# Rows of a norm's reciprocals by four transposes, and another order in the last half of the final norm

## The chip, the cores and the metric

The kernel runs on one core of one Trainium2 chip. A NeuronCore has TensorE (matmuls and transposes into PSUM; the profile calls it PE, and its weight loads PEld), VectorE (DVE), ScalarE (ACT), GpSimd (POOL) and SyncE (SP, which here only issues DMAs). The metric is the device time of one execution in microseconds, as the median of several runs. Before the change the median of 3 runs is 1398.92 us (1397.98 to 1399.54).

## The reference

A decoder trunk of two layers over 512 tokens and a model width of 1024: a gated DeltaNet layer, a channel mixer, a shared K/V projection with sliding-window attention, a second channel mixer, and a final norm. What the change touches is the norm, whose divisors are made four times after the first layer's mixer (the K/V and the query norm share theirs):

```python
def rmsnorm(x, w):
    xf = x.astype(jnp.float32)
    y = xf * lax.rsqrt(jnp.mean(xf * xf, axis=-1, keepdims=True) + EPS)
    return (y * w.astype(jnp.float32)).astype(x.dtype)
```

It divides each token by the root of the mean of its 1024 squares and weighs each feature. Ahead of a projection the kernel multiplies the weighed but undivided activations and divides the product afterwards, token by token; at the end the output itself is the norm.

## The kernel before, in words

Activations lie turned: `h[0]` to `h[7]`, each 128 features on the partitions and the 512 tokens along the row (`T` = 512, `NC` = 4 blocks of 128 tokens, `P` = 128). Every large product is made of three matmuls a block of 128 features (L165, L166, L167: upper part times upper part, and two mixed ones), into one of three PSUM banks tagged `d`. Other banks are tagged `g` (two), `s` (two) and `p` (one).

The reciprocals of the roots. `rstd_cols` squares the eight rows on ScalarE (L860), adds them on VectorE into `acc` (L864), and sums over the 128 partitions with four small matmuls against a column of ones (L867), so that the 512 sums stand as four columns of 128 tokens; root (L869, ScalarE) and reciprocal (L870, VectorE) give `rt`, 128 x 4. The products, however, have the tokens along the row. `rstd_rows` therefore turns the four columns into a row that is the same on all partitions: VectorE multiplies the identity by each column (L876), which gives four diagonal blocks in the tile `st3` (`st` in the profile), and one matmul with a block of ones (L883) sums each column of that diagonal over the partitions; ScalarE copies the bank to the tile `p6s` (L885), and VectorE multiplies the products by it (L911 in the channel mixer, L1284 in the attention). This is done three times: in the first channel mixer (near 525 us), in the attention (near 887 us) and in the second channel mixer (near 1037 us). `st3` is at other times a third buffer for weights of the down projections, which are loaded from L1032 by SP's queue, and on whose parts VectorE first makes sums (L1067).

The down projections and the DeltaNet's output projection are made in a form of seven block products (L1051 to L1053), for which VectorE adds and subtracts parts of weights and of activations first; in the output projection these activations come back from DRAM (`yd`, L1152 on SP) into the tiles `sz` and `zl`.

The final norm. `ffn(1, ..., last=True)` leaves out the last 128 features of its down projection and calls `final`, which interleaves them with the norm. The first seven rows are weighed (L1207) and their squares added into `acc` there, and the four transposes of the first 512 features of each block of tokens (`front`) are made before. The last row's product comes in two halves of 256 tokens (`CUTS`). Each half, once its product is added (L1258), is finished by `finish(u)`: the last row is weighed (L1233) and squared (L1234, `sq7`), the other four rows of each block are transposed (`back`), the squares summed in columns (L1239, first `acc`, then `sq7`, for each block), root and reciprocal taken (L1240, L1241), and the two halves of each block of output rows scaled by `rt`, the front one on VectorE (L1248), the back one on ScalarE (L1246), and sent out from SP's queue (L1249), 256 KB each.

The order of the work on each engine is set by a scheduler from the order in the code, priorities and buffers; `behind(later, earlier)` ties one instruction behind another on an engine without a wait, and `together` keeps several instructions of TensorE in one piece.

Of the kernel before, what the change touches and what calls it, by code (L numbers as in the profile page):

```python
# [11 lines left out]
AF = mybir.ActivationFunctionType  # L12
ALU = mybir.AluOpType
# [4 lines left out]
P = 128  # L18
T = 512
NC = T // P  # L20
D = 1024
KD = D // P
EPS = 1e-6
# [21 lines left out]
def kernel(  # L45
# [27 lines left out]
    V, S, G, PE, SP = nc.vector, nc.scalar, nc.gpsimd, nc.tensor, nc.sync  # L73
# [9 lines left out]
    def nm(s):  # L83
        cnt[0] += 1
        return f"{s}_{cnt[0]}"
# [24 lines left out]
    def row(tag, dt=F32, n=T):  # L110
        return main.tile([P, n], dt, tag=tag, bufs=ROWS[tag], name=nm(tag))
# [4 lines left out]
    def bank(tag):  # L116
        return psum.tile([P, T], F32, tag=tag, bufs=BANKS[tag], name=nm(tag))

    def const(shape, dt=F32, s="c"):
        return cp.tile(list(shape), dt, name=nm(s))  # L120
# [58 lines left out]
    def behind(later, earlier):  # L179
        info = mybir.DependencyInfo(mybir.DependencyClass.NoSync, mybir.DependencyReason.DATA)  # L180
        tc.add_manual_dep(later.ins, earlier.ins.name, info, reason="order of issue")
# [3 lines left out]
    def together(makes, *after):  # L185
        first = None
        for make in makes:
            if first is None:
                first = make()
                for a in after:  # L190
                    behind(first, a)
            else:
                with tc.high_priority(JUMP):
                    behind(make(), first)
# [16 lines left out]
    for i in range(2):  # L211
        cs = slice(HQK * P + i * P, HQK * P + (i + 1) * P)
# [4 lines left out]
    ident = const([P, P], s="ident")  # L217
# [3 lines left out]
    ones = const([P, P], s="ones")  # L221
    V.memset(ones[:], 1.0)
    epsc = const([P, 1], s="eps")
    V.memset(epsc[:], EPS)
    onec = ones[:, 0:1]
# [4 lines left out]
    def columns(parts, n, s, q=SP, tag="acc", place="g"):  # L230
        st = row(tag, n=P)
        r = 0
        for ap in parts:
            k = ap.shape[0]
            q.dma_start(st[r : r + k, :], ap)
            r += k
        ps = bank(place)
        PE.transpose(ps[:, :n], st[:n, :], ident[:n, :n])
        t = const([P, n], s=s)
        V.tensor_copy(t[:], ps[:, :n])  # L240
        return t
# [11 lines left out]
        q=S,  # L253
# [11 lines left out]
    xh, xl = [], []  # L265
    for k in range(KD):
        ps = bank("g") if k % 2 else bank("s")
# [68 lines left out]
    for c in range(NC):  # L336
        cs = slice(c * P, (c + 1) * P)
        V.tensor_tensor_scan(R[32:48, cs], ones[32:48, 0:P], sp_r[32:48, cs], 0.0, op0=ALU.mult, op1=ALU.add)
    for c in range(NC):
        cs = slice(c * P, (c + 1) * P)  # L340
# [38 lines left out]
    def hc(ap):  # L379
# [36 lines left out]
    onw_c = columns(  # L416
        [
            fconv_rows[0, 128:132, :],
            fconv_rows[1, 128:132, :],
            a_out_norm_w,  # L420
            final_norm_w.rearrange("(r c) -> r c", c=P),
        ],
        17,
        "onwc",
        tag="f",
# [351 lines left out]
    for pos, word in enumerate(" ".join(ORDER).split(), 1):  # L777
        name, _, later = word.partition("@")
        a, n = name[0], [int(d) for d in name[1:]]
# [33 lines left out]
    def nxt(role, tags):  # L813
        turn[role] = turn.get(role, -1) + 1
        return tags[turn[role] % len(tags)]

    def r2(role, dt=F32):
        return row(nxt(role, ROLES[role]), dt)
# [4 lines left out]
    def third_stage():  # L823
        return main.tile([P, 6, 256], F32, tag="st3", bufs=1, name=nm("st3"))
# [25 lines left out]
    for m in range(KD):  # L850
        x3 = xrows[m].rearrange("p (c e) -> p c e", c=NC)
        SP.dma_start(x3, x[0, :, m * P : (m + 1) * P].rearrange("(c p) e -> p c e", p=P))
        pt = bank("g")
        turn_row(pt, xrows[m])
        S.copy(hT[m], pt[:])
    def rstd_cols(h):
        acc = None
        for k in range(KD):
            sq = r2("sum" if acc is None else "hsq")
            S.activation(sq[:], h[k], AF.Square)  # L860
            if acc is None:
                acc = sq
            else:
                V.tensor_tensor(acc[:], acc[:], sq[:], op=ALU.add)  # L864
        ps = bank("g")
        for c in range(NC):
            PE.matmul(ps[:, c : c + 1], acc[:, c * P : (c + 1) * P], onec, start=True, stop=True)  # L867
        rt = const([P, NC], s="rt")
        S.activation(rt[:], ps[:, 0:NC], AF.Sqrt, bias=epsc[:, 0:1], scale=1.0 / D)  # L869
        V.reciprocal(rt[:], rt[:])  # L870
        return rt

    def rstd_rows(h):
        rt = rstd_cols(h)
        dg = third_stage()[:, 0:2, :].rearrange("p k c -> p (k c)")
        V.tensor_tensor(  # L876
            dg[:].rearrange("p (c t) -> p c t", c=NC),
            ident[:].unsqueeze(1).to_broadcast([P, NC, P]),
            rt[:].unsqueeze(2).to_broadcast([P, NC, P]),
            op=ALU.mult,  # L880
        )
        ps = bank("g")
        PE.matmul(ps[:], ones[:], dg[:], start=True, stop=True)  # L883
        r = r2("rstd")
        S.copy(r[:], ps[:])  # L885
        return r
# [11 lines left out]
    def ffn(l, h, last=False):  # L898
        wup, wdn = ffn_w_up[l], ffn_w_down[l]
        uh, ul = normed(h, NFFN + 8 * l)  # L900
        rs = rstd_rows(h)

        def tap(j, t):
# [274 lines left out]
    for m2 in range(KD // 2):  # L1178
        srcs = [tiles_of(a_w_out[0], 1024 * u, 8, 256 * m2) for u in range(2)]
        sts = [load_stage(a_w_out[0], 1024 * u, 8, 256 * m2) for u in range(2)]  # L1180
        if m2 < 2:
            for j in range(2):
                m = 2 * m2 + j
                ps = bank("d")
# [15 lines left out]
    def final(h, last_down):  # L1200
        hw, acc = [], None
        for k in range(KD):
            t = r2("xh")
            hw.append(t)
            if k == KD - 1:
                break
            V.tensor_scalar(t[:], h[k], onw_c[:, 9 + k : 10 + k], None, op0=ALU.mult)  # L1207
            sq = r2("sum" if acc is None else "hsq")
            S.activation(sq[:], h[k], AF.Square)
            if acc is None:  # L1210
                acc = sq
            else:
                V.tensor_tensor(acc[:], acc[:], sq[:], op=ALU.add)

        def turned(hf, c, tag):
            pt = bank(tag)
            for k in range(4):
                PE.transpose(pt[:, k * P : (k + 1) * P], hw[4 * hf + k][:, c * P : (c + 1) * P], ident[:])
            return pt

        CUTS = [(0, 2), (2, 4)]
        parts = [bank("d") for _ in CUTS]
        S.activation(warm[:], acc[:, 0:1], AF.Sqrt)
        front = [turned(0, c, t) for c, t in enumerate(["s", "s", "p", "g"])]
        h7, w7 = h[KD - 1], hw[KD - 1]
        sq7 = r2("hsq")
        rt = const([P, NC], s="rt")
        ts = [slice(a * P, b * P) for a, b in CUTS]

        def finish(u):  # L1230
            c0, c1 = CUTS[u]
            cs = slice(c0, c1)
            V.tensor_scalar(w7[:, ts[u]], h7[:, ts[u]], onw_c[:, 16:17], None, op0=ALU.mult)  # L1233
            S.activation(sq7[:, ts[u]], h7[:, ts[u]], AF.Square)  # L1234
            back = [turned(1, c, "s" if u and c % 2 else "d") for c in range(c0, c1)]
            ps = bank("g")
            for c in range(c0, c1):
                for x in (acc, sq7):
                    PE.matmul(ps[:, c : c + 1], x[:, c * P : (c + 1) * P], onec, start=x is acc, stop=x is sq7)  # L1239
            S.activation(rt[:, cs], ps[:, cs], AF.Sqrt, bias=epsc[:, 0:1], scale=1.0 / D)  # L1240
            V.reciprocal(rt[:, cs], rt[:, cs])  # L1241
            for c in range(c0, c1):
                for hf, pt in enumerate((front[c], back[c - c0])):
                    y = r2("xl")
                    if hf:
                        S.activation(y[:], pt[:], AF.Copy, scale=rt[:, c : c + 1])  # L1246
                    else:
                        V.tensor_scalar(y[:], pt[:], rt[:, c : c + 1], None, op0=ALU.mult)  # L1248
                    SP.dma_start(out[0, c * P : (c + 1) * P, hf * T : (hf + 1) * T], y[:])  # L1249

        n = len(CUTS)
        for u in range(n):
            ps = parts[u][:, 0 : ts[u].stop - ts[u].start]
            last_down(ps, ts[u], 0)
            if u > 0:
                finish(u - 1)
            last_down(ps, ts[u], 1)
            V.tensor_tensor(h7[:, ts[u]], h7[:, ts[u]], ps, op=ALU.add)  # L1258
        finish(n - 1)


    Vp = main.tile([P, NC, 256], F32, tag="m32", bufs=1, name="Vp")
# [281 lines left out]
```

## Time and profile before

| | us |
|---|---|
| median of 3 runs | 1398.92 (1397.98 to 1399.54) |
| the profiled execution | 1399.55 |
| its span, from the first to the last instruction | 1397.4 |
| TensorE busy | 1374.6 |
| VectorE busy | 1144.3 |
| ScalarE busy | 765.6 |

The profile takes one execution apart. Rows of the timeline give the start and the length in us, engine, source line, operation, output tile and input tiles, shapes and, in brackets, how long the engine had been idle and what ended that. Lengths of matmuls overlap, so that what one costs is read from the distance of starts. `xN` at the end of a row counts instructions that were merged into it; a float32 matmul (not a transpose) is two instructions.

### The profile page before, as it was taken

How to read it: one execution, taken by the hardware profiler on the slowest of the kernel's cores; microseconds unless marked ns; L12 is line 12 of the kernel's file. 1: busy time of each engine (PE TensorE's matmuls, PEld its weight loads, DVE VectorE, ACT ScalarE, POOL GpSimd, SP SyncE). 2: the span in 40 equal slices, each digit the busy share in tenths (PEclk: the TensorE clock that was granted, in tenths of full speed). 3: DMA queues.
4: the chain of work that ended last, by engine and by line, in shares of the span. 5: the costliest groups of instructions: out<-in, count | busy, mean ns of one | idle time of the engine just before them, and what ended most of it. 6: DMA issues, size and time to landing. Idle time of an engine off the chain costs nothing.

```text
span 1397.4 us, 22194 instructions
## 1 busy us (share of the span) xinstructions
PE 1374.6 (98%) x8514; PEld 1171.0 (84%) x8514; DVE 1144.3 (82%) x2153; ACT 765.6 (55%) x1482; POOL 15.2 (1%) x33
## 2 busy tenths in 40 slices
PE   7999999999999999999999999999999999999998
PEld 5788887888887898888988889877788889988897
DVE  4896896978967998879968899788668889878996
ACT  7766465757557455444344445677545444444543
POOL 1000000000100000000000000000000000000000
PEclk9999999999999999999999999999999999999999
DMA  5234154162567334221343223312132221432222
GB/s 162 83 114 134 50 173 141 64 197 91 171 192 225 127 119 140 94 88 52 130 151 121 76 84 114 121 62 69 61 113 91 91 95 63 146 106 80 96 76 76
DMA packets 164029, 154.97 MB, mean 111 GB/s; under 512 B 24340, under 2 KB 150869, under 8 KB 163925
## 3 DMA queue, kind: packets, MB, share of 16 engines
q1 hardware_dynamic: 161666, 153.37, 34.3%
q8 instruction: 67, 1.10, 0.3%
q10 hardware_dynamic: 2259, 0.20, 0.1%
q14 instruction: 37, 0.30, 0.1%
HBM read 136.74 MB, written 15.75 MB: 109 GB/s over the span
## 4 chain that ended last, share of the span: by engine, by line
PE 90%; DVE 4%; ACT 3%; DMA 2%; issue 1%; SPq 0%; DVEq 0%; ACTq 0%
PE d L165 19%; PE d L167 19%; PE d L166 19%; PE g L201 2%; PE d L1053 2%; PE d L1051 2%; PE d L1052 2%; PE s L1053 1%; PE s L1051 1%; PE s L1052 1%; PE d L1307 1%; PE d L1311 1%; PE d L1309 1%; PE g L1053 1%; PE g L1052 1%; PE g L1051 1%
## 5 line engine op out<-in xcount | busy, mean ns | idle before, releaser
L166 PE MATMUL d<-xl,whi 128*128 128x512 f32 x1128 | 443.0, 395 | 0.0
L165 PE MATMUL d<-xh,whi 128*128 128x512 f32 x1128 | 442.6, 395 | 0.4 <-DVE va L1284 0.3
L167 PE MATMUL d<-xh,wlo 128*128 128x512 f32 x1128 | 442.5, 394 | 0.0
L135 ACT CAST whi<-stage 128x1024 fp32r<-128x1024 f32 (+2 forms) x238 | 231.6, 977 | 224.9 <-PE d L166 129.3
L136 DVE TENSOR_TENSOR wlo<-stage,whi 128x1024 fp32r<-128x1024 f32 (+2 forms) x238 | 268.1, 1129 | 51.8 <-ACT whi L135 50.5
L165 PEld LDWEIGHTS d<-xh,whi 128*128 128x128 f32 x1128 | 211.7, 188 | 44.8 <-DVE va L1284 0.7
L167 PEld LDWEIGHTS d<-xh,wlo 128*128 128x128 f32 x1128 | 211.7, 188 | 44.5 <-DVE wlo L136 0.7
L166 PEld LDWEIGHTS d<-xl,whi 128*128 128x128 f32 x1128 | 211.7, 188 | 43.4 <-issue 0.7
L283 DVE SCALAR_TENSOR_TENSOR acc<-d,cwc,acc 128x511 f32<-128x511 f32 (+2 forms) x96 | 70.2, 738 | 5.2 <-ACT acc L280 4.5
L933 ACT ACTIVATE dt<-dt 128x512 f32<-128x512 f32 x44 | 27.8, 632 | 80.2 <-DVE dt L916 80.2
L911 DVE TENSOR_TENSOR sz<-d,p6s 128x512 f32<-128x512 f32 x58 | 39.9, 688 | 37.6 <-PE d L167 35.3
L916 DVE SCALAR_TENSOR_TENSOR va<-sz,fcw,va 128x511 f32<-128x511 f32 (+1 forms) x58 | 43.4, 747 | 1.7 <-ACT va L914 0.9
L916 DVE SCALAR_TENSOR_TENSOR dt<-sz,fcw,dt 128x511 f32<-128x511 f32 (+1 forms) x58 | 43.3, 746 | 1.7 <-ACT dt L914 0.9
L564 DVE TENSOR_TENSOR sT<-sT,p6s 64x31 f32<-64x31 f32 (+15 forms) x124 | 40.8, 329 | 1.6
L1376 ACT ACTIVATE dt<-dt,sm 128x256 f32<-128x256 f32 (+1 forms) x64 | 30.1, 471 | 21.5 <-DVE sm L1359 21.5
L558 DVE TENSOR_TENSOR p6s<-sN,sT 64x31 f32<-64x31 f32 (+15 forms) x124 | 40.6, 327 | 1.5
L135 ACT CAST whi<-st 128x768 fp32r<-128x768 f32 (+1 forms) x30 | 23.8, 792 | 31.5 <-PE g L1052 8.6
L911 DVE TENSOR_TENSOR zl<-d,p6s 128x512 f32<-128x512 f32 x30 | 20.6, 688 | 23.0 <-PE d L167 22.7
L693 ACT ACTIVATE rq<-o 128x128 f32<-128x128 f32 x64 | 19.0, 297 | 35.7 <-DVE o L688 26.1
L935 DVE TENSOR_TENSOR va<-dt,va 128x512 f32<-128x512 f32 x44 | 30.4, 690 | 1.3
L136 DVE TENSOR_TENSOR wlo<-st,whi 128x768 fp32r<-128x768 f32 (+1 forms) x30 | 26.9, 900 | 2.1 <-ACT whi L135 1.7
L914 ACT ACTIVATE dt<-sz,normc,fcw 128x512 f32<-128x512 f32 x29 | 23.6, 815 | 7.3 <-DVE sz L911 7.1
(859 smaller groups left out, 2975.6 us busy)
## 6 DMA issues: line engine op xcount, KB each, us to landing
stage<-in_ffn_w_up_dram SPq DMA_DIRECT2D x44, 1024.0 KB, 5.0
stage<-in_a_w_in_dram SPq DMA_DIRECT2D x23, 1024.0 KB, 5.2
stage<-in_ffn_w_down_dram SPq DMA_DIRECT2D x16, 768.0 KB, 4.9
stage<-in_a_w_out_dram SPq DMA_DIRECT2D x8, 1024.0 KB, 6.0
st<-in_ffn_w_down_dram SPq DMA_DIRECT2D x8, 768.0 KB, 5.2
zd<-sz SPq DMA_DIRECT2D x16, 256.0 KB, 2.0
od<-o SPq DMA_DIRECT2D x16, 256.0 KB, 2.4
stage<-in_b_w_q_dram SPq DMA_DIRECT2D x4, 1024.0 KB
```

Of the source, the lines that this page charges most:

```text
L135: S.copy(hi[:, :kt, :m], src)
L136: V.tensor_tensor(lo[:, :kt, :m], src, hi[:, :kt, :m].bitcast(F32), op=ALU.subtract)
L165: PE.matmul(ps, hi[:, k, :m], xh[k], start=first and k == 0, stop=False)
L166: PE.matmul(ps, hi[:, k, :m], xl[k][:], start=False, stop=False)
L167: done.append(PE.matmul(ps, lo[:, k, :m], xh[k], start=False, stop=last and k == kt - 1))
L283: V.scalar_tensor_tensor(acc[:, d:], ps[:, : T - d], col, acc[:, d:], op0=ALU.mult, op1=ALU.add)
L564: V.tensor_tensor(Tm[:, s + 1 : 32, 0:m], Tm[:, s + 1 : 32, 0:m], tv, op=ALU.subtract)
L911: V.tensor_tensor(u[:], ps[:], rs[:], op=ALU.mult)
L916: V.scalar_tensor_tensor(acc[:, d:], u[:, : T - d], tap(2 - d, t), acc[:, d:], op0=ALU.mult, op1=ALU.add)
L1051: PE.matmul(ps, w[0][:, wk, :], hi, start=first and k == 0, stop=False, **kw)
L1052: PE.matmul(ps, w[0][:, wk, :], lo, start=False, stop=False, **kw)
L1053: PE.matmul(ps, w[1][:, wk, :], hi, start=False, stop=k == n - 1, **kw)
```

## The change

It has three parts.

1. In `rstd_rows` the multiplication of the identity and the matmul with ones go. In their place stand four transposes, each of one column of `rt` that is broadcast to 128 columns, into the four quarters of the same bank. They are kept in one piece. The tile `st3` is no longer used there.
2. In `finish` the order changes. In both halves the transposes of the last row's blocks stand behind the sums of squares. In the second half `acc` is summed by itself, into a bank of its own; VectorE divides these sums by 1024 and adds epsilon into a new tile `rest`; the sums of `sq7` go to a bank `d`; the root is taken block by block, with `rest` as its bias, and so is the reciprocal. The back half rows are scaled ahead of the front ones, and the front half row of the second block is scaled in the second half, behind the weighing.
3. The very last half row (back, last block) is issued from ScalarE's queue in place of SP's.

```diff
     def rstd_rows(h):
         rt = rstd_cols(h)
-        dg = third_stage()[:, 0:2, :].rearrange("p k c -> p (k c)")
-        V.tensor_tensor(
-            dg[:].rearrange("p (c t) -> p c t", c=NC),
-            ident[:].unsqueeze(1).to_broadcast([P, NC, P]),
-            rt[:].unsqueeze(2).to_broadcast([P, NC, P]),
-            op=ALU.mult,
+        ps = bank("g")
+        together(
+            [
+                lambda c=c: PE.transpose(ps[:, c * P : (c + 1) * P], rt[:, c : c + 1].to_broadcast([P, P]), ident[:])
+                for c in range(NC)
+            ]
         )
-        ps = bank("g")
-        PE.matmul(ps[:], ones[:], dg[:], start=True, stop=True)
...
+        def finish(u, left):
+            cs, at = range(*CUTS[u]), slice(*CUTS[u])
             S.activation(sq7[:, ts[u]], h7[:, ts[u]], AF.Square)
+            weighed = V.tensor_scalar(w7[:, ts[u]], h7[:, ts[u]], onw_c[:, 16:17], None, op0=ALU.mult)
+            if left:
+                behind(left(), weighed)
+            back = {c: bank("s" if u and c % 2 else "d") for c in cs}
+            for c in cs:
+                turn_into(back[c], 1, c, range(3))
+            ps = bank("d" if u else "g")
+            if u:
+                sums = bank("g")
+                columns_of(sums, acc, cs)
+                V.tensor_scalar(rest[:, at], sums[:, at], 1.0 / D, EPS, op0=ALU.mult, op1=ALU.add)
+                summed = columns_of(ps, sq7, cs)
...
+            for c in cs:
+                behind(turn_into(back[c], 1, c, [3]), summed[-1])
+            if u:
+                for c in cs:
+                    S.activation(rt[:, c : c + 1], ps[:, c : c + 1], AF.Sqrt, bias=rest[:, c : c + 1], scale=1.0 / D)
+                    V.reciprocal(rt[:, c : c + 1], rt[:, c : c + 1])
...
+                q = S if hf and c == NC - 1 else SP
+                q.dma_start(out[0, c * P : (c + 1) * P, hf * T : (hf + 1) * T], y[:])
...
+            for c in cs:
+                half_row(c, 1, back[c])
+                if u or c == 0:
+                    half_row(c, 0, front[c])
+            return lambda: half_row(1, 0, front[1])
```

Three places show how the instructions stand. The names are tiles with a running number; L numbers of the changed kernel are its own.

TensorE in the attention, around the row of reciprocals, before. `g` is the bank of the row, `d` a bank of the products:

```order
L166 MATMUL d_8834<-xl_8702,whi_8835 128x512
L167 MATMUL d_8834<-xh_8701,wlo_8836 128x512
L165 MATMUL d_8834<-xh_8705,whi_8835 128x512
L883 MATMUL g_8816<-st_1402_8814,ones_88 128x512
L166 MATMUL d_8834<-xl_8706,whi_8835 128x512
L167 MATMUL d_8834<-xh_8705,wlo_8836 128x512
```

The same place now:

```order
L165 MATMUL d_8836<-xh_8702,whi_8837 128x512
L166 MATMUL d_8836<-xl_8703,whi_8837 128x512
L167 MATMUL d_8836<-xh_8702,wlo_8838 128x512
L878 MATMUL g_8815<-ident_81,rt_8812 128x128 x4
L165 MATMUL d_8836<-xh_8706,whi_8837 128x512
L166 MATMUL d_8836<-xl_8707,whi_8837 128x512
```

Four transposes stand where the matmul with ones stood, one matmul earlier (three in each channel mixer). The column sums ahead of them stand two matmuls later than before, since VectorE now sums weights (L1067, for the second channel mixer) ahead of the last square's addition.

The end of TensorE's queue, second half of the final norm, before. `ol` holds the sums of seven squares (`acc` in the code), the tile `acc` the last square, and the fourth `xh` of a group is the weighed last row:

```order
L1218 MATMUL s_13685<-ident_81,xh_13554 128x128
L1239 MATMUL g_13690<-ones_88,ol_13527 128x1
L1218 MATMUL d_13680<-ident_81,xh_13559 128x128
L1218 MATMUL s_13685<-ident_81,xh_13559 128x128
L1239 MATMUL g_13690<-ones_88,acc_13583 128x1
L1239 MATMUL g_13690<-ones_88,ol_13527 128x1
L1239 MATMUL g_13690<-ones_88,acc_13583 128x1
```

The same place now:

```order
L1215 MATMUL s_13685<-ident_81,xh_13557 128x128
L1219 MATMUL g_13693<-ones_88,ol_13530 128x1 x2
L1219 MATMUL d_13692<-ones_88,acc_13587 128x1 x2
L1215 MATMUL d_13684<-ident_81,xh_13562 128x128
L1215 MATMUL s_13685<-ident_81,xh_13562 128x128
```

The sums of the seven squares come first and those of the last one ahead of the two last transposes. VectorE at the same place, before, from the first half's reciprocal on:

```order
L1241 RECIPROCAL rt_13584<-rt_13584 128x2
L1248 TENSOR_SCALAR xl_13653<-s_13563,rt_13584 128x512
L1248 TENSOR_SCALAR xl_13659<-s_13568,rt_13584 128x512
L1258 TENSOR_TENSOR pz_4516<-pz_4516,d_13561 128x256
L1233 TENSOR_SCALAR xh_13559<-pz_4516,onwc_367 128x256
L1241 RECIPROCAL rt_13584<-rt_13584 128x2
L1248 TENSOR_SCALAR xl_13697<-p_13573,rt_13584 128x512
L1248 TENSOR_SCALAR xl_13703<-g_13578,rt_13584 128x512
```

And now:

```order
L1262 RECIPROCAL rt_13588<-rt_13588 128x2
L1269 TENSOR_SCALAR xl_13660<-s_13566,rt_13588 128x512
L1287 TENSOR_TENSOR pz_4516<-pz_4516,d_13564 128x256
L1237 TENSOR_SCALAR xh_13562<-pz_4516,onwc_367 128x256
L1269 TENSOR_SCALAR xl_13681<-s_13567,rt_13588 128x512
L1247 TENSOR_SCALAR rest_13586<-g_13693 128x2
L1259 RECIPROCAL rt_13588<-rt_13588 128x1 x2
L1269 TENSOR_SCALAR xl_13708<-p_13568,rt_13588 128x512
L1269 TENSOR_SCALAR xl_13714<-g_13569,rt_13588 128x512
```

The second scaling of the first half has moved behind the addition and the weighing of the second half, and the sums with epsilon stand between it and the reciprocals.

SP's queue in the DeltaNet's output projection, before:

```order
L852 DMA f_4528<-in_x_dram 128x4x128
L1152 DMA sz_4760<-yd 128x512
L1152 DMA sz_4761<-yd 128x512
L1152 DMA zl_4776<-yd 128x512
L1152 DMA sz_4777<-yd 128x512
```

And now:

```order
L852 DMA f_4528<-in_x_dram 128x4x128
L1150 DMA sz_4760<-yd 128x512
L1030 DMA st_1056_6489<-in_ffn_w_down_dram 128x6x256
L1150 DMA sz_4761<-yd 128x512
L1150 DMA zl_4776<-yd 128x512
L1150 DMA sz_4777<-yd 128x512
```

The first weights of the first channel mixer's down projection, which stood behind four loads of its up projection, are now loaded here. In the same way the first such load of the second channel mixer now stands ahead of the loads of the query weights.

More of the change, by code (lines that the diff above doesn't have):

```diff
@@ L1213, in final, with turn_into, columns_of @@
                 V.tensor_tensor(acc[:], acc[:], sq[:], op=ALU.add)
[L1215 to L1219, printed above, removed]
+        def turn_into(pt, hf, c, ks):
+            for k in ks:
+                last = PE.transpose(pt[:, k * P : (k + 1) * P], hw[4 * hf + k][:, c * P : (c + 1) * P], ident[:])
+            return last
+        def columns_of(ps, x, cs):
+            one = lambda c: PE.matmul(ps[:, c : c + 1], x[:, c * P : (c + 1) * P], onec, start=True, stop=True)
+            return [one(c) for c in cs]
         CUTS = [(0, 2), (2, 4)]
@@ L1223, in final @@
         S.activation(warm[:], acc[:, 0:1], AF.Sqrt)
-        front = [turned(0, c, t) for c, t in enumerate(["s", "s", "p", "g"])]
+        front = [bank(t) for t in ("s", "s", "p", "g")]
+        for c, pt in enumerate(front):
+            turn_into(pt, 0, c, range(4))
+        rest = const([P, NC], s="rest")
         h7, w7 = h[KD - 1], hw[KD - 1]
@@ L1228, in final @@
         ts = [slice(a * P, b * P) for a, b in CUTS]
[L1230 to L1233, printed above, removed]
+        def finish(u, left):
+            cs, at = range(*CUTS[u]), slice(*CUTS[u])
             S.activation(sq7[:, ts[u]], h7[:, ts[u]], AF.Square)
[L1235 to L1249, printed above, removed]
@@ new lines, in finish @@
+            weighed = V.tensor_scalar(w7[:, ts[u]], h7[:, ts[u]], onw_c[:, 16:17], None, op0=ALU.mult)
[10 more added lines that the diff above has]
+                summed = columns_of(ps, sq7, cs)
+            else:
+                for c in cs:
+                    for x in (acc, sq7):
+                        one = x[:, c * P : (c + 1) * P]
+                        summed = [PE.matmul(ps[:, c : c + 1], one, onec, start=x is acc, stop=x is sq7)]
@@ new lines, in finish, with half_row @@
+            for c in cs:
[4 more added lines that the diff above has]
+                    V.reciprocal(rt[:, c : c + 1], rt[:, c : c + 1])
+            else:
+                S.activation(rt[:, at], ps[:, at], AF.Sqrt, bias=epsc[:, 0:1], scale=1.0 / D)
+                V.reciprocal(rt[:, at], rt[:, at])
+            def half_row(c, hf, pt):
+                y = r2("xl")
+                if hf:
+                    scaled = S.activation(y[:], pt[:], AF.Copy, scale=rt[:, c : c + 1])
+                else:
+                    scaled = V.tensor_scalar(y[:], pt[:], rt[:, c : c + 1], None, op0=ALU.mult)
+                q = S if hf and c == NC - 1 else SP
+                q.dma_start(out[0, c * P : (c + 1) * P, hf * T : (hf + 1) * T], y[:])
+                return scaled
@@ L1251, in final @@
+            for c in cs:
+                half_row(c, 1, back[c])
+                if u or c == 0:
+                    half_row(c, 0, front[c])
+            return lambda: half_row(1, 0, front[1])
         n = len(CUTS)
@@ L1255, in final @@
             if u > 0:
-                finish(u - 1)
+                left = finish(u - 1, None)
             last_down(ps, ts[u], 1)
             V.tensor_tensor(h7[:, ts[u]], h7[:, ts[u]], ps, op=ALU.add)
-        finish(n - 1)
+        finish(n - 1, left)
     Vp = main.tile([P, NC, 256], F32, tag="m32", bufs=1, name="Vp")
```

## The prediction

> **What bounds the kernel now.** First the page: its span, and the chain of waits followed back from the end.
>
> ```profile
> span 1397.4 us, 22194 instructions
> ...
> PE 90%; DVE 4%; ACT 3%; DMA 2%; issue 1%; SPq 0%; DVEq 0%; ACTq 0%
> ```
>
> Nine tenths of the chain is TensorE itself. So a step counts in full if it stands in TensorE's queue or delays it, and behind the last matmul counts whatever ends last; a VectorE instruction elsewhere is free while TensorE does not run out of work. I then read the timeline of TensorE at the three places where the rows of reciprocals are made, and all engines and the DMA view over the last 12 us.
>
> TensorE's timeline at the middle place, in the attention (start, duration, line, tile, idle time in brackets):
>
> ```profile
> 886.94 0.40 PE L165 MATMUL d<-xh,whi 128*128 128x512 f32 x1
> 887.17 1.02 PE L883 MATMUL g<-st,ones 128*128 128x512 f32 x2
> 887.63 0.80 PE L166 MATMUL d<-xl,whi 128*128 128x512 f32 x1
> 888.27 0.40 PE L167 MATMUL d<-xh,wlo 128*128 128x512 f32 x1
> ...
> 889.60 0.50 PE L165 MATMUL d<-xh,whi 128*128 128x512 f32 x1 [0.25 <-DVE va L1284]
> ```
>
> Starts, not durations, give the cost in a stream of matmuls. An ordinary one takes 0.23 us from start to start (886.94 to 887.17). From L165 to L167 lie 1.33 us where two such steps would be 0.46: the diagonal times ones, one matmul in two float32 passes, costs 0.87 us of TensorE. The last row shows TensorE waiting 0.25 us for the product va, which needs the row of reciprocals. All three places have the same two passes:
>
> ```profile
> L883 PE MATMUL g<-st,ones x6: 590/592/595, 525.4 to 1037.9; 128*128 128x512 f32 x6
> ```
>
> **The change part by part. The rows of reciprocals.** Removed: 3 x 0.87 us of TensorE and a VectorE multiplication at each place. Added: four transposes a place. The trace has no transpose of a broadcast column, but it has ordinary ones of the same shape, 128x128 float32 in one pass, at the start of the final norm (eight, then four more):
>
> ```profile
> 1378.13 1.04 PE L1218 MATMUL s<-ident,xh 128*128 128x128 f32 x8
> 1379.00 0.60 PE L1218 MATMUL p<-ident,xh 128*128 128x128 f32 x4
> ```
>
> Eight take 0.87 us from start to start, 0.109 each; four take 0.44. So a place saves 0.87 - 0.44 = 0.43, three save 1.30 us. The bounds of the unknown part, a weight load that reads one element 128 times: no cheaper than 0.109, since each still streams the identity, and no dearer than its own length without any overlap, 0.27 (0.60 for four, less three starts of 0.109). I take 0.109, because only the address step differs.
>
> The Trainium skill ("TensorE: Matmul & The Clock Gate", Part 4: PE-mode transpose) speaks against this part: it gives a transpose of 128x128 in a kernel about 275 ns, most of it access latency. By that figure four would cost 1.1 us, more than what they replace, and the three places would lose some 0.7 us. This trace shows such a number too, but as the length of one instruction; the starts are 0.109 apart.
>
> On VectorE the place loses the multiplication L876:
>
> ```profile
> 884.77 0.18 DVE L870 RECIPROCAL rt<-rt 128x4 f32<-128x4 f32 x1 [0.43 <-ACT rt L869]
> 884.99 0.69 DVE L876 TENSOR_TENSOR st<-ident,rt 128x512 f32<-128x512 f32 x1
> 888.85 1.29 DVE L1284 TENSOR_TENSOR va<-d,p6s 128x512 f32<-128x512 f32 x2 [3.17 <-ACT p6s L885]
> ```
>
> VectorE was idle for 3.17 us right after, so its 0.69 is worth nothing by itself. But the transposes stand one to three matmuls earlier and are 0.43 shorter, so the row reaches va about 0.7 us sooner (0.23 + 0.43), while TensorE comes to its wait only 0.43 sooner: the 0.25 us there go. The new order puts a weight sum (L1067, moved here from the second channel mixer) ahead of the last square:
>
> ```profile
> 854.40 0.55 DVE L1067 TENSOR_TENSOR st<-st 128x384 f32<-128x384 f32 x1
> ```
>
> and the column sums two matmuls later (0.46). The reciprocals are then there near 885.4 (884.77 + 0.46 + 0.18), and the transposes would start one matmul before L883's 887.17, near 886.9: 1.5 us of cover. At the other two places TensorE waits for nothing. Sum of this part: 1.30 + 0.25 = 1.55 us.
>
> **The queues.** The diagonal no longer holds the tile st, so two weight loads into it are issued earlier. One comes from behind the first up loads to between the loads of yd; this is SP's timeline there, the last transposes that read the old contents of st, and further on an idle time of VectorE and TensorE's next wait:
>
> ```profile
> 445.79 5.89 SPq L1152 DMA_DIRECT2D sz<-yd  x2
> ```
> ```profile
> 447.55 1.07 PE L201 MATMUL g<-ident,st 128*128 128x128 f32 x8
> ```
> ```profile
> 485.87 1.23 DVE L136 TENSOR_TENSOR wlo<-stage,whi 128x1024 fp32r<-128x1024 f32 x1 [0.99 <-ACT whi L135]
> ```
> ```profile
> 495.76 0.38 PE L1053 MATMUL d<-kT,wlo 128*128 128x256 f32 x1 [0.62 <-DVE wlo L136]
> ```
>
> The two loads of sz are issued at 445.8 and near 451.3 (the pair ends at 451.68). The moved load has to wait for the transposes, until 448.6, and is issued into that gap, so nothing behind it on SP waits. It moves 768 KB ahead of the second sz. VectorE has 0.99 us of idle time at 485.87, of which the weight sum that also moves there takes 0.55; so a delay of up to 0.44 costs nothing, and a longer one goes to TensorE one for one. I cost it at 0. The other load (of the second channel mixer) moves into the attention ahead of the query weights, where st is free before their buffers are.
>
> **The last half.** TensorE, VectorE, ScalarE from the end of the last product:
>
> ```profile
> 1388.71 0.28 PE L962 MATMUL d<-S,wlo 128*128 128x256 f32 x1
> ...
> 1389.49 0.28 PE L1239 MATMUL g<-ones,ol 128*128 128x1 f32 x2
> 1390.17 0.33 PE L1218 MATMUL d<-ident,xh 128*128 128x128 f32 x1 [0.40 <-DVE xh L1233]
> ...
> 1390.58 0.36 PE L1239 MATMUL g<-ones,ol 128*128 128x1 f32 x2
> 1390.81 0.36 PE L1239 MATMUL g<-ones,acc 128*128 128x1 f32 x2
> ```
> ```profile
> 1387.99 1.41 DVE L1248 TENSOR_SCALAR xl<-s,rt 128x512 f32<-128x512 f32 x2
> 1389.31 0.41 DVE L1258 TENSOR_TENSOR pz<-pz,d 128x256 f32<-128x256 f32 x1
> 1389.76 0.35 DVE L1233 TENSOR_SCALAR xh<-pz,onwc 128x256 f32<-128x256 f32 x1
> 1391.50 0.17 DVE L1241 RECIPROCAL rt<-rt 128x2 f32<-128x2 f32 x1 [1.39 <-ACT rt L1240]
> ```
> ```profile
> 1389.76 0.42 ACT L1234 ACTIVATE acc<-pz 128x256 f32<-128x256 f32 x1 [0.50 <-DVE pz L1258]
> 1391.21 0.26 ACT L1240 ACTIVATE rt<-g,eps 128x2 f32<-128x2 f32 x1 [1.03 <-PE g L1239]
> 1391.70 0.69 ACT L1246 ACTIVATE xl<-d,rt 128x512 f32<-128x512 f32 x1 [0.23 <-DVE rt L1241]
> ```
>
> The product is there at 1388.99, but the addition L1258 starts at 1389.31, behind two scalings. One of these moves behind the weighing, so the addition starts 0.3 sooner, near 1389.0, and the square near 1389.45, ending at 1389.87. TensorE does the sums of acc meanwhile: two columns at 0.22 each (1390.58 to 1390.81), from 1389.49 to 1389.93; then the two of the square until 1390.37, where before they ended at 1391.03. So TensorE alone would bring the root 0.66 us forward. But the new bias of the root is read by VectorE, behind the moved scaling: 1389.8 + 0.70 (half of 1.41) + some 0.2 for the small instruction (near the reciprocal's 0.17) = 1390.7. The root starts near 1390.75 in place of 1391.21. Two single roots instead of one put the second 0.2 later, but the first back row needs only the first: it starts near 1391.25 instead of 1391.70. Gain 0.45; bounds 0 and 0.66, and a loss only if VectorE came to the small instruction 0.5 us later than this.
>
> Does the end follow? SP's first issue of the last four half rows, its whole series, and the DMA view from 1386.0 in 40 slices of 0.285 us:
>
> ```profile
> 1392.42 0.33 SPq L1249 DMA_DIRECT2D out_dram<-xl  x1
> ```
> ```profile
> 1388.70 5.52 SPq L1249 DMA_DIRECT2D out_dram<-xl  x8
> ```
> ```profile
> DMA  0000000000004999999997000499999999500000
> GB/s 0 0 0 0 0 0 0 0 0 0 0 0 165 424 381 431 388 417 395 417 388 273 0 0 0 194 417 388 417 410 403 431 374 431 216 0 0 0 0 0
> ```
>
> The last four rows go out from 1393.1 to 1395.8 without a gap at about 400 GB/s: 4 x 256 KB in 2.7 us. They are bound by the transfer, and the end follows its start, 0.45 us sooner. The half row moved out of the first group leaves in the gap before (TensorE and VectorE rows: ready near 1390.5), and delays nothing. Issuing the last one from ScalarE then saves nothing, as its bytes wait for the DMA engines anyway: 0. It costs nothing either: no instruction stands behind it on ScalarE.
>
> **Sum.** 1.30 + 0.25 + 0.45 = 2.0 us. The profiled execution took 1399.55 us, its span 1397.4 and 2.15 around it; it would take 1397.55. It lies 0.63 above the median of 1398.92, from which the same sum gives 1396.9.
>
> **The rivals.** *Transposes that do not overlap*, because the broadcast loads can't run ahead: 4 x 0.27 = 1.09 a place in place of 0.87, three times 0.22 lost; 0.25 + 0.45 - 0.66 leaves 0: 1398.9. For it: no such load in the trace; against it: twelve close transposes. 0.08. The Trainium skill's figure above would give about the same. *The tail stays*, since the bias waits longer on VectorE or the rows leave no sooner: 1.55 us, 1397.4. 0.17. *The tail is bound by issue*: SP's last issue ends at 1394.22 (1388.70 + 5.52), the ScalarE queue has its row by about 1392.6, and the end moves by 1 us instead of 0.45: 1396.3. Against it the gapless slices. 0.13. *VectorE starves* at the loads of yd, the slower side: the profile's page gives the moved load 5.2 us to its landing:
>
> ```profile
> st<-in_ffn_w_down_dram SPq DMA_DIRECT2D x8, 768.0 KB, 5.2
> ```
>
> If sz had to wait for all of it, VectorE would be late by 5.2, less 0.44 of cover; 4.8 less the 2.0 gained gives 1401.7. It decides from a delay of 2.44 us on. Against it: the load starts almost 3 us before the second sz is issued. 0.05. *No effect*, the median within 0.5 of before: 0.04. *More than counted*: waits such as the 0.62 at 495.76 go too, 2.9 us or more, 1395.9: 0.05. My forecast keeps 0.48.
>
> **Numbers.** 0.2%, about what a measurement can tell from no change, is 2.8 us, 1396.1. Faster by more: the last rival, two fifths of issue-bound, and a little of the forecast's scatter (the three runs lie 1.6 us apart): 0.15. Slower: 0.05. Within: 0.80. The range runs from 1395.7 (bounds of the tail and the last rival) to 1398.9 (no overlap), and leaves out the starved VectorE and the ends of the scatter.
>
> **What would show it.** Right: four transposes between steady matmuls with 0.44 us between where L883 had 0.87; no wait behind the first va; the second addition near 0.05 us after its product; the first root gated by VectorE; the last four rows without a gap over 2.7 us. Wrong: starts of the transposes 0.2 or more apart; a wait of TensorE between 474 and 496 beyond 0.62; a gap between the last rows, or a last row that lands later than 2.7 us after the first began.

## The result, and the profile after

The changed kernel is slower: 1413.99 us (1411.07 to 1414.31) against 1399.23 us (1398.0 to 1400.5) for the kernel before, run on the same chip; ratio 1.0101, 95% interval 1.0083 to 1.0118. The forecast was 1396.9, with 1398.9 as the upper end of the range. The profiled execution took 1414.19 us. Its page:

```profile
span 1412.0 us, 22206 instructions
...
PE 91%; DVE 3%; ACT 2%; DMA 2%; issue 1%; ACTq 0%; DVEq 0%; SPq 0%
```

14.6 us more of span, and TensorE still is nine tenths of the chain. So the time is on TensorE, but not in waits. This is TensorE's list of waits in the kernel after, longest first (engine, line, releaser: us in total, times, longest):

```profile
PE g L238 <- DMA acc<-in_ffn_conv_b_dram: 9.5, 1, 9.5
PE d L1049 <- ACT whi L158: 2.0, 2, 1.0
PE d L165 <- ACT whi L135: 1.1, 3, 0.5
```

The first is the start of the program. Before, it took this long:

```profile
PE g L238 <- DMA xt<-in_x_dram: 8.6, 1, 8.6
```

The start takes anything from 7.9 to 10.0 us in the traces of this case. All of TensorE's waits over 0.15 us together are 17.8 us now, 16.1 before, and 15.0 to 18.4 in the traces of the experiments, so they account for nothing near 14 us. The places that the change touches are all well, too. The row of reciprocals in the attention, on TensorE:

```profile
895.19 0.40 PE L167 MATMUL d<-xh,wlo 128*128 128x512 f32 x1
895.42 0.60 PE L878 MATMUL g<-ident,rt 128*128 128x128 f32 x4
895.78 0.48 PE L165 MATMUL d<-xh,whi 128*128 128x512 f32 x1
896.10 0.39 PE L166 MATMUL d<-xl,whi 128*128 128x512 f32 x1
...
897.03 0.40 PE L167 MATMUL d<-xh,wlo 128*128 128x512 f32 x1
897.42 0.50 PE L165 MATMUL d<-xh,whi 128*128 128x512 f32 x1
```

From L167 to L166 lie 0.91 us for two ordinary steps and the four transposes; less two steps of 0.233 they cost 0.44. And the end, all engines, then the DMA view from 1400.6 in 40 slices of 0.285 us:

```profile
1403.76 0.28 PE L960 MATMUL d<-S,wlo 128*128 128x256 f32 x1
1404.08 0.42 DVE L1287 TENSOR_TENSOR pz<-pz,d 128x256 f32<-128x256 f32 x1 [0.44 <-PE d L960]
1405.46 0.15 DVE L1247 TENSOR_SCALAR rest<-g 128x2 f32<-128x2 f32 x1
1405.71 0.41 ACT L1258 ACTIVATE rt<-d,rest 128x1 f32<-128x1 f32 x2 [0.76 <-DVE rest L1247]
1406.26 0.69 ACT L1267 ACTIVATE xl<-d,rt 128x512 f32<-128x512 f32 x1
```
```profile
DMA  0000000000000199999999940699999999900000
```

The last product starts 8.24 us before the end of the span (1412.0 - 1403.76); before it was 8.69 (1397.4 - 1388.71). The tail is 0.45 us shorter.

Where, then, are 14.6 us and the 2 that were saved? In the matmuls that nobody touched. Groups by line and shape, two of the three lines of the large projections, of before and then of after (count | busy us, mean ns of one):

```profile
L166 PE MATMUL d<-xl,whi 128*128 128x512 f32 x1120 | 439.8, 395 | 0.0
L165 PE MATMUL d<-xh,whi 128*128 128x512 f32 x1120 | 439.4, 395 | 0.4 <-DVE va L1284 0.3
```
```profile
L165 PE MATMUL d<-xh,whi 128*128 128x512 f32 x1120 | 444.9, 399 | 0.5 <-ACT whi L135 0.3 <-ACT xh L175 0.2
L166 PE MATMUL d<-xl,whi 128*128 128x512 f32 x1120 | 443.8, 398 | 0.0
```

Lengths went up by 4 ns in 395; a stream is priced by its starts, so here are two rows of TensorE's timeline ten products apart, inside a stream without a gap, of before and then of after:

```profile
599.83 0.39 PE L167 MATMUL d<-xh,wlo 128*128 128x512 f32 x1
...
602.10 0.39 PE L165 MATMUL d<-xh,whi 128*128 128x512 f32 x1
```
```profile
599.86 0.40 PE L165 MATMUL d<-xh,whi 128*128 128x512 f32 x1
...
602.19 0.40 PE L166 MATMUL d<-xl,whi 128*128 128x512 f32 x1
```

2.27 and 2.33 us for ten products. The median of all steps behind a 512-column product is 227 ns before and 234 after. Three stretches of 35 us in which TensorE never idles, of before and after (us, PE busy (count), granted clock, DMA share, GB/s); the second is a stage of 256-column products:

```profile
595.00:630.00 35.00, 35.00 (x157) 1.00 0.24 78
665.00:700.00 35.00, 35.00 (x294) 1.00 0.35 118
1050.00:1085.00 35.00, 35.00 (x157) 1.00 0.28 91
```
```profile
595.00:630.00 35.00, 35.00 (x152) 1.00 0.28 91
665.00:700.00 35.00, 35.00 (x298) 1.00 0.42 136
1050.00:1085.00 35.00, 35.00 (x152) 1.00 0.26 88
```

The granted clock is 1.00 in all of them, so it isn't the clock. The 512-column products are slower in every stage, also at 595 to 630, hundreds of microseconds away from anything the change touches; the 256-column ones are, if anything, faster (median 118 ns for 120). Summing the steps from one start to the next over the whole trace, for the products with whi or wlo as weights: the 3,576 of 512 columns that read xh or xl took 838.2 us before and 855.7 after (+17.5), the 414 other 512-column ones 100.1 and 102.2 (+2.1), the 2,139 256-column ones 261.7 and 258.0 (-3.7). Together +15.9; less the 2.0 us that the change saves, 13.9 of the 14.6; the 0.7 left is no more than the 1.0 by which the start differs.

What do all of these share, that the change could reach? Their operands' places in memory. The tile rest is new. It lies in the pool const, and the pool main, which holds every product's columns (its input of 512 or 256 columns: xh, xl, sy, kT and so on), begins where const ends. A tile's place in the built programs, in bytes from the start of a partition:

```
               before    after
rt (last)       10720    10752
rest                -    10720
sy (main)       10752    10784
xh (main)       39424    39456
xl (main)       55808    55840
whi (weights)  204288   204288
wlo (weights)  216576   216576
```

Its 16 bytes take 32, and all of main moves up by them, while the pool of the weights, which is laid out from the other end, stays. Before, main began at 21 x 512 and the weights' pool at 367 x 512: two empty tiles, gap_x in const (line 78) and gap_w in weights (line 305), have sizes that put both there.

### The profile page after: what moved, and what is told of

Read it like the earlier page. It is cut to its first block, busy times and chain, and to the rows that moved or that the text cites. A ratio compares the mean times of both kernels' runs of the same rounds, so it can differ in the third digit from the quotient of the medians.

```text
span 1412.0 us, 22206 instructions
## 1 busy us (share of the span) xinstructions
PE 1387.8 (98%) x8520; PEld 1162.9 (82%) x8520; DVE 1143.3 (81%) x2152; ACT 765.4 (54%) x1483; POOL 15.2 (1%) x33
## 4 chain that ended last, share of the span: by engine, by line
PE 91%; DVE 3%; ACT 2%; DMA 2%; issue 1%; ACTq 0%; DVEq 0%; SPq 0%
PE d L165 20%; PE d L167 20%; PE d L166 19%; PE g L201 2%; PE d L1051 2%; PE d L1049 2%; PE d L1050 2%; PE s L1051 1%; PE s L1049 1%; PE s L1050 1%; PE d L1336 1%; PE d L1340 1%; PE d L1338 1%; PE g L1051 1%; PE g L1050 1%; PE g L1049 1%
## 5 line engine op out<-in xcount | busy, mean ns | idle before, releaser
L165 PE MATMUL d<-xh,whi 128*128 128x512 f32 x1128 | 448.1, 399 | 0.5 <-ACT whi L135 0.3
L167 PE MATMUL d<-xh,wlo 128*128 128x512 f32 x1128 | 447.7, 399 | 0.5 <-DVE wlo L136 0.5
L166 PE MATMUL d<-xl,whi 128*128 128x512 f32 x1128 | 446.9, 398 | 0.0
L165 PEld LDWEIGHTS d<-xh,whi 128*128 128x128 f32 x1128 | 211.1, 187 | 51.4 <-ACT whi L135 0.9
L167 PEld LDWEIGHTS d<-xh,wlo 128*128 128x128 f32 x1128 | 211.1, 187 | 50.7 <-DVE wlo L136 1.2
L166 PEld LDWEIGHTS d<-xl,whi 128*128 128x128 f32 x1128 | 211.2, 187 | 48.8
```

The costliest lines, as they stand in the source:

```text
L165: PE.matmul(ps, hi[:, k, :m], xh[k], start=first and k == 0, stop=False)
L166: PE.matmul(ps, hi[:, k, :m], xl[k][:], start=False, stop=False)
L167: done.append(PE.matmul(ps, lo[:, k, :m], xh[k], start=False, stop=last and k == kt - 1))
```

## The experiments

**Theory**: the place of main, not any instruction, costs the 16 us. **Rivals**: the four transposes, the weight loads that they let move ahead, or the order of the end. Four kernels take the two apart.

*The changed kernel without the shift.*

```diff
-        rest = const([P, NC], s="rest")
-        rt = const([P, NC], s="rt")
+        both = const([P, 2 * NC], s="rt")
+        rt, rest = both[:, 0:NC], both[:, NC : 2 * NC]
```

> The changed kernel with one edit: the small tile rest gets no room of its own; rt is made twice as wide and rest is its second half. Every instruction stays; in the built program every tile of the pools main and const then starts at the byte where it starts in the kernel before, while in the changed kernel every tile of main starts 32 bytes higher (sN at 10784 for 10752). Theory (the shift of the operands' addresses makes the 512-column products slower, and the change itself brings the gain that was predicted): 1397 us, ratio 0.998 to 0.9995, and a steady stretch again has about 156 matmuls in 35 us for the 152 of the changed kernel. Rivals (the four transposes, the moved loads, or the new order of the end make it slower): about 1414 us, ratio 1.010, 152 matmuls.

Measured: 1395.72 us, before 1397.85; ratio 0.9987 (0.9974 to 1.0000). The steady stretch and the group of L165:

```profile
595.00:630.00 35.00, 35.00 (x156) 1.00 0.21 69
```
```profile
L165 PE MATMUL d<-xh,whi 128*128 128x512 f32 x1120 | 439.6, 395 | 0.2
```

All instructions of the change are in this kernel, and it is at the ratio that was expected of it, though the interval reaches to no gain.

*The kernel before with the shift alone.*

```diff
+        const([P, 4], s="spare")
         h7, w7 = h[KD - 1], hw[KD - 1]
```

> The kernel before with one line more: a tile of 128 x 4 fp32 in the pool const, made at the place where the changed kernel makes rest, and never written or read. No instruction changes; every tile of main starts 32 bytes higher. Theory (addresses): 1416 us, that is the 1414.0 of the changed kernel and the 2.0 us that its edits save; ratio 1.010 to 1.014; 152 matmuls in 35 us of a steady stretch. Rivals (any cause in the instructions): 1399 us, ratio 1.000 within 0.001, 156 matmuls.

Measured: 1414.75 us, before 1397.85; ratio 1.0123 (1.0096 to 1.0150).

```profile
595.00:630.00 35.00, 35.00 (x152) 1.00 0.28 91
```

A tile that nothing reads or writes costs what the change cost, and the 2 us that its edits save. The rivals fall.

*The rows alone*: before, with L876 and L883 replaced by

```diff
+        together([lambda c=c: PE.transpose(ps[:, c * P : (c + 1) * P],
+                  rt[:, c : c + 1].to_broadcast([P, P]), ident[:]) for c in range(NC)])
```

> The kernel before with the first part of the change alone: the four transposes for the product with ones, at all three places; no tile moves. Theory (addresses, and the sum of the prediction): 1.3 us less for three rows and 0.25 us less for the wait of the attention's first product, 1397.7 us, ratio 0.9989. Rival that puts the loss on the transposes or on the two weight loads that move earlier: over 1405 us. Rival that transposes gain nothing: 1399.2 us, ratio 1.000.

Measured: 1396.06 us, before 1397.85; ratio 0.9989 (0.9977 to 1.0002), the ratio of the sum. The interval also holds no gain.

*The end alone*: the kernel of the first experiment with the old rows.

> The kernel before with the second and third part alone (the order of the last sums, the last half row issued by ScalarE), and rest in the second half of rt, so that no tile moves. Theory (addresses, and the sum of the prediction): 0.45 us less, 1398.8 us, ratio 0.9997. Rival that puts the loss on the end of the kernel: it can't touch the products ahead of it, so at most the last 40 us change; over 1405 us only if the end itself is 6 us longer, which the trace of the changed kernel does not show.

Measured: 1397.73 us, before 1397.85; ratio 1.0001 (0.9989 to 1.0013). 0.45 us is 0.0003, less than this can show; its trace has the last product at 1387.67 of a span of 1395.8, so a tail of 8.13 us for 8.69. The tail is 8.7 to 8.8 us in the ten traces with the old end and 8.1 to 8.3 in the four with the new one: it is shorter, though the times of whole runs can't tell it.

The next four ask what it is about the place: where the columns lie (A), or how far from the weights (B), and in what unit.

*Both pools 32 bytes higher*: the unused tile, and

```diff
-    wpool.tile([P, 120], F32, tag="gap", bufs=1, name="gap_w")
+    wpool.tile([P, 112], F32, tag="gap", bufs=1, name="gap_w")
```

> The kernel before with the unused tile of 128 x 4 fp32 in const (main 32 bytes higher) and the empty tile gap_w 8 columns narrower, which puts the weights' pool 32 bytes higher too. The distance between products' columns (main) and their weights is that of the kernel before, only the place of both differs. Theory A (the place of the columns alone counts): slow as the kernel with the unused tile, about 1415 us, 512-column products 233 to 234 ns apart. Theory B (the distance between columns and weights counts): as the kernel before, 1398 to 1399 us, 227 ns apart.

Measured: 1399.17 us, before (in this and the next three) 1397.82; ratio 1.0018 (1.0008 to 1.0028); median step of 512 columns 227 ns.

```profile
1050.00:1085.00 35.00, 35.00 (x156) 1.00 0.29 91
```

*The weights alone, 32 bytes lower*: gap_w 128 columns wide in place of 120.

> The kernel before with the empty tile gap_w 8 columns wider: the weights' pool lies 32 bytes lower, main stays where it was. Theory A (the place of the columns alone counts): as the kernel before, 1398 to 1399 us, 512-column products 227 ns apart. Theory B (the distance between columns and weights counts): about 1415 us, 234 ns apart. A third theory (each operand has its own price for its place, the weights' load too): something between, or above 1415 with both moved.

Measured: 1413.28 us; ratio 1.0113 (1.0098 to 1.0128); 234 ns.

```profile
1050.00:1085.00 35.00, 35.00 (x152) 1.00 0.32 104
```

B: with every column of main in its old place the products are slow, and with every column displaced they are as before, when the weights move along. What counts is the distance. (The 0.0018 that the kernel with both pools displaced stays above before, 1.4 us by the medians and 2.5 by the ratio, is not in the products: the steps of xh and xl sum to 838.7 us, of before to 838.2. It isn't explained.)

*64 and 96 bytes*: the unused tile 16 and 24 columns wide.

> The kernel before with an unused tile of 128 x 16 fp32 in const: main 64 bytes higher. If the place counts in units of 64 bytes (or the distance does), it is as the kernel before: 1398 to 1399 us, 227 ns from one 512-column product to the next. If it counts in units of 128 bytes or more, it is slower, 1415 us if any place but a full unit costs the same.

Measured: 1402.28 us; ratio 1.0031 (1.0018 to 1.0044); 229 ns.

```profile
1050.00:1085.00 35.00, 35.00 (x155) 1.00 0.28 91
```

> The kernel before with an unused tile of 128 x 24 fp32 in const: main 96 bytes higher. If the place counts in units of 64 bytes, it is slow like the one with 32 bytes, about 1415 us, 234 ns. If it counts in units of 32 bytes, none of these could be slow. If the price grows with the distance from a full unit, it is over 1415.

Measured: 1419.60 us; ratio 1.0156 (1.0141 to 1.0171); 232 ns. So neither a unit of 64 bytes nor a price that grows with the distance: 64 costs 6 us of xh and xl steps, 32 and 96 cost 19 each. That 96 comes out slower than 32 as a whole lies mostly in the 256-column products, which gain 5 us at 32 and 1 at 96. The last four ask whose columns count, and how large the unit is.

*All of main behind xl shifted, the rest in place*: the kernel of the first experiment, with

```diff
         xh.append(h)
         xl.append(l)
+    main.tile([P, 8], F32, tag="gap_m", bufs=1, name="gap_m")
```

> The changed kernel with rest inside rt (as in the first experiment), and an empty tile of 128 x 8 fp32 in main behind the rows xl: xh, xl, sy, nt and acc keep their place, all tiles of main behind them lie 32 bytes higher. Theory (each product is priced by the distance of its own columns from the weights): 512-column products that read xh, xl and sy stay at 227 ns, the 230 or so that read kT, qT, at, ktok, vt go to 234 (1.6 us more), and the 1,400 256-column products that read those tiles go from 120 to 117 or 118 ns (3.3 us less). In all 1.7 us under the first experiment: 1394, ratio to before 0.9975. Rival (the whole pool's shift counts, by something other than the product's own columns): 512-column products of xh and xl slow down too, over 1405 us.

Measured: 1395.41 us, before 1397.42; ratio 0.9988 (0.9977 to 0.9999). Steps of xh and xl 227 ns (836.2 us in all); of the other 512-column products 233 (99.4 us in the first experiment, 101.3 here); of the 256-column products on shifted tiles 118 (173.9 to 172.3), on unshifted ones 120. Each product went with its own columns, as expected. The net gain of 1.7 us did not come: the sums say 1.9 lost and 1.6 won. I had priced the 256-column products by their medians, and their sums move less. These sums tell little, though: among kernels with all distances 0 the first lies anywhere from 99.4 to 101.5 us, the second from 173.9 to 175.0. It is the medians that show which products moved.

*xh and xl alone shifted*: before, with an empty tile of 8 columns ahead of xh and one of 120 columns behind xl.

> The kernel before with an empty tile of 32 bytes in main ahead of the rows xh and one of 480 bytes behind the rows xl: xh and xl alone lie 32 bytes higher, what follows lies 512 bytes higher. Theory (a product's own columns, their distance counted within 512 bytes or less): the 3,576 512-column products that read xh and xl go to 234 ns, 18 us more by the traces of before and after; the 256-column ones of other tiles stay at 120 ns: 1416 us, ratio 1.013, more than the changed kernel, since the 3.6 us that the 256-column products gain there are missing. Rival (the tiles of other stages matter, or what VectorE and ScalarE write at the same time): nearer to 1399 us.

Measured: 1413.97 us, before (in this and the next two) 1397.42; ratio 1.0117 (1.0103 to 1.0131). xh and xl 234 ns and 856.3 us, 18.1 more; the other 512-column products 227, the 256-column ones 120.

```profile
595.00:630.00 35.00, 35.00 (x152) 1.00 0.28 91
```

*128 and 512 bytes*: the unused tile 32 and 128 columns wide.

> The kernel before with an unused tile of 128 x 32 fp32 in const: all of main 128 bytes higher. If the distance counts within units of 128 bytes: 1398 us, 227 ns for 512 columns, 120 ns for 256. If within a larger unit: between 1398 and 1420 us, with spacings other than 227 and 120 ns.

Measured: 1415.64 us; ratio 1.0127 (1.0111 to 1.0142); 232 ns.

> The kernel before with an unused tile of 128 x 128 fp32 in const: all of main 512 bytes higher, the distance to the weights a multiple of 512 bytes as before. If the distance counts within 512 bytes or a divisor of it: 1398 us, 227 and 120 ns. If the absolute distance counts: another time.

Measured: 1398.50 us; ratio 1.0003 (0.9991 to 1.0015); 227 and 120 ns.

```profile
1050.00:1085.00 35.00, 35.00 (x156) 1.00 0.28 91
```

512 bytes more are free, and 128 are not. A distance of 256 was not tried, so the price may come back every 512 bytes or every 256. All in one table; the distance is that of the columns' places above the weights', as a remainder of 512 bytes, and the last two columns sum the steps from start to start in each trace. In brackets stand the tiles other than xh and xl:

```
kernel             distance    median ns, 512   xh,xl 512, us   all 256, us
before                 0            227             838.2          261.7
both pools +32         0            227             838.7          261.7
main +512              0            227             840.4          261.8
rest inside rt         0            227             837.5          260.9
after                 32            234             855.7          258.0
unused tile, +32      32            234             857.1          256.5
weights -32           32            234             857.0          256.6
xh, xl alone +32      32 (0)        234 (227)       856.3          260.3
behind xl alone +32    0 (32)       227 (233)       836.2          259.2
main +64              64            229             844.2          258.7
main +96              96            232             857.1          260.5
main +128            128            232             855.0          260.6
```

Medians and sums do not rank 32 and 96 alike, since at 96 some three steps in ten take 237 or 238 ns. The mean of the xh and xl steps up to 300 ns is 227.7 at 0, 229.5 at 64, 232.5 at 128, 233.3 at 32 and 233.4 at 96.

## Why the prediction was wrong

*The step that failed* is the sum, "1.30 + 0.25 + 0.45 = 2.0 us". It counted the instructions that the change removes, adds and moves, and took the price of the other 8,500 matmuls as given. No term, and no rival, stood for the new tile rest as a thing that takes up room. The term that was missing is +15.9 us in the trace after; with the tile's room taken away (first experiment) the rest of the sum comes out, 0.9987 measured (0.9974 to 1.0000) for 0.9986. That interval alone would not tell the sum from no gain; the traces show its terms one by one. The list of what would prove the forecast wrong had no spacing of untouched products on it either, and that is the one that moved.

*The rows* (1.30 and 0.25): right. 0.44 us a place (0.43 to 0.45 at all nine places of the kernel after, of the first experiment and of the rows alone), and before the product that waits for va the gap is 0.39 us from start to start (897.03 to 897.42), where it was 0.64 (from 888.96, the row below from the timeline of before, to the 889.60 that the prediction quotes). The idle time that the profile named is gone, though 0.16 us over an ordinary step remain, so "the 0.25 us there go" holds for the amount and not for the whole wait. With the rows alone the idle time is gone as well, and with the unused tile alone it is still 0.24 us, so it is the rows that took it away.

```profile
888.96 0.39 PE L167 MATMUL d<-xh,wlo 128*128 128x512 f32 x1
```

*Transposes that do not overlap*: did not happen. A transpose of the broadcast column is 272 ns long, and the four together 0.60, so their starts are 0.11 apart.

```profile
L878 PE MATMUL g<-ident,rt x12: 271/272/273, 527.0 to 1046.5; 128*128 128x128 f32 x12
```

The Trainium skill's some 275 ns ("TensorE: Matmul & The Clock Gate", Part 4: PE-mode transpose) agrees with this as a length (its text speaks of bf16 data, these are float32); as a price in a stream it would be two and a half times too much.

*The tail* (0.45): right, and by the chain that was named. The second addition starts 0.04 us behind its product (1404.08, 1403.76 + 0.28), the root waits for VectorE's rest, and the first back row starts 2.50 us behind the last product's start for 2.99 before (1391.70 - 1388.71). The last four rows go out in ten slices without a gap. The rival in which issue bounds the tail would have shown 1 us; the tail gave 0.45.

*VectorE starved at the loads of yd*: no. TensorE's wait for wlo, 0.62 at 495.76 before, isn't there after: between 439 and 664 us TensorE has no wait over 0.15 us. Elsewhere the waits for wlo are these, the first in the block products, the second in a projection at 716 us:

```profile
PE d L1051 <- DVE wlo L136: 0.6, 2, 0.3
PE d L167 <- DVE wlo L136: 0.5, 1, 0.5
```

That the 0.62 went is no merit of the change: no other trace of this case has it at this place, with the old rows or the new ones.

*What stays open* is why the distance counts. In the stream the load of the next product's weights starts with the product itself; the timeline of the kernel after, of TensorE's products and of its loads:

```profile
611.99 0.40 PE L166 MATMUL d<-xl,whi 128*128 128x512 f32 x1
...
611.99 0.19 PEld L167 LDWEIGHTS d<-xh,wlo 128*128 128x128 f32 x1
```

So one instruction reads columns while the other reads 128 fp32 weights in each partition, which is 512 bytes, a shift that was found to be free. The loads themselves do not get longer, the products do (minimum, median and maximum in ns, of before and then of after):

```profile
L167 PEld LDWEIGHTS d<-xh,wlo x1128: 122/188/334, 15.2 to 1331.7; 128*128 128x128 f32 x187, 128*48 128x48 f32 x1
L167 PE MATMUL d<-xh,wlo x1128: 387/389/632, 15.7 to 1331.9; 128*128 128x512 f32 x187, 128*48 128x512 f32 x1
```
```profile
L167 PEld LDWEIGHTS d<-xh,wlo x1128: 120/187/246, 15.1 to 1346.2; 128*128 128x128 f32 x187, 128*48 128x48 f32 x1
L167 PE MATMUL d<-xh,wlo x1128: 387/396/583, 15.3 to 1346.4; 128*128 128x512 f32 x187, 128*48 128x512 f32 x1
```

That the two reads meet in the memory would give a price that depends on their distance alone; it is an inference, no run here separates the load from the product. The Trainium skill ("SBUF — State Buffer", A bandwidth-pool intuition that's wrong) gives TensorE a second, independent read port for weight loads, by which I would have expected no such price; here the same instructions differ by 3% with the distance, and the measurement decides.

## What to carry to other kernels

A new tile is part of a change, however small: compare the places of all operands of the dominant instruction before and after, and keep them, by room that is there already (rest inside rt costs nothing) or by an empty tile that fills up to the old place. When the profile after shows no new wait and still a longer span, compare the step from start to start of instructions that were not touched, in a stage far from the change. Empty tiles of odd sizes in a kernel can be holding such a distance.

The lowest three kernels here are the changed one with rest inside rt (0.9987, 0.9974 to 1.0000), the same with the tiles behind xl 32 bytes higher (0.9988, 0.9977 to 0.9999) and the rows alone (0.9989, 0.9977 to 1.0002); between them nothing is shown.

## What the runs showed of the hardware

The price of a product of type fp32r (so the row of wlo in the prediction calls it) hangs on the distance between its columns and the weights, as a remainder of 512 bytes or perhaps of 256: 512 columns every 227 ns at 0, 229 at 64, 232 at 96 and 128, 234 at 32, by the median. The price isn't the same for all widths: 256 columns take 120 ns at 0, 117 to 118 at 32 and 64, and 119 to 120 at 96 and 128, so the place that slows one stage speeds up another. Where columns and weights lie as such, each by 32 bytes off a multiple of 512, costs the products nothing as long as both are off alike (227 ns).

A transpose of 128x128 float32 is 272 ns long, and four in a row, each of one column read 128 times, start 0.11 us apart and cost 0.44 us of TensorE together.
